# A list scheduler's hand-over times, and a choice of ScalarE or VectorE for each copy

## The chip, the cores and the metric

The kernel runs on one core of a Trainium2 chip. The time is that of the whole program on the device in microseconds (us), as a median over runs. The profile is of one execution.

## The reference

The program computes two transformer blocks, one after the other, on 512 tokens of width 1024 in float32. The first block has two layers; each is a feed-forward, a mixer, and a second feed-forward. The mixer of the first layer is an mLSTM with memory cross-attention, that of the second a dilated attention with memory cross-attention.

```python
for layer in range(DEPTH):
    x = x + 0.5 * swiglu(rms_norm(x, ffn1_norm[layer]), ...)
    h = rms_norm(x, mix_norm[layer])
    mix = mlstm_mixer(h, mem_n, ...) if layer < N_A_LAYERS else dilated_mixer(h, mem_n, k_sh, v_sh, ...)
    x = x + mix
    x = x + 0.5 * swiglu(rms_norm(x, ffn2_norm[layer]), ...)
```

The second block has two layers as well. Each scales and shifts its input by a learned modulation, projects it to everything that its three mixers need, and runs an RWKV recurrence in both directions, an attention with grouped heads and rotated queries and keys (with softmax), and an attention over neighbouring tokens. A context of 256 tokens goes through the same steps ahead of the 512.

```python
h_lat = x * (1.0 + scale[:, None]) + shift[:, None]
ru_l, rg_l, aq_l, ak_l, av_l, ag_l, nq_l, nk_l, nv_l, ng_l = jnp.split(h_lat @ w_in, SPLIT_POINTS, axis=-1)
_, _, ys_l = _rwkv_bidir(rin_l, S_f, S_b)                  # RWKV, both directions
gq_l = _apply_axial_rope(gqa_q(aq_l), cos, sin)            # rotated queries
ya_l = _block_attention(gq_l..., concat(gk_c, gk_l), concat(gv_c, gv_l))
yn_l = _neighbourhood_attention(nq_l, nk_l, nv_l, nk_c, nv_c, rpb)
y_l = concat([yr_l * silu(rg_l), ya_l * silu(ag_l), yn_l * silu(ng_l)]) @ w_out
x = _layer_norm(DEEPNORM_ALPHA * x + gate[:, None] * y_l, ln_g, ln_b)
```

## The kernel before

**Matrix products.** Activations lie with the channels on the 128 partitions and the 512 tokens along the free axis. Each float32 operand of a large product is split into a high and a low part; the three products high x high, high x low and low x high are added up in PSUM. A split is two instructions: a copy that rounds to the high part (ScalarE, `t<-raw` for weights), and a subtraction for the low part (VectorE, `t<-raw,t`). `raw` tiles are weights as loaded, `t` tiles hold 128x512 values, `ps` are the eight PSUM banks, `uv`, `S`, `big` and `tmp` belong to RWKV, and `s8`, `s16`, `s32`, `s64` are small tiles of scalars (the profile shows them as `s`).

**The program is a list first.** `Prog` runs through the two blocks and only records operations (`Op`): engine, method, operands. `weave` mixes the lists of parts that may run side by side: RWKV on the context beside the second feed-forward of the first block, and attention beside RWKV in each layer of the second block (`layer_mix`). `dependences` finds who must wait for whom. `schedule` then finds the order, and `emit` writes the instructions in that order. Since one line of `emit` issues everything, nearly every row of the profile names line 583; operations are told apart by engine, tile names and shapes.

**What sets the order.** `simulate` is a list scheduler. It keeps, for each of five engines, the time at which it comes free, and a time at which each operation is ready: the end of what it waits for plus `LATENCY` of that engine, plus `INTO_PE` if it is TensorE that waits. `_cost` gives each operation's length. At each step it takes the operation that can start first, by priority among those that are ready, and gives its tiles a free slot out of `SLOTS`. A change of TensorE's tile size is charged with `RETILE`, and on TensorE an operation of the same tile size may go ahead of others as long as their priorities lie within `STAY` us. `schedule` runs it backward through the program, takes the times as priorities for a run forward, and repeats this three times. On the chip each engine works through its own list in order and waits by semaphores; none of the planner's times reach the chip, only the order and the slots.

**Places that the prediction's steps touch.** `qstat` (lines 885 to 895) sums squares of a head on TensorE, reads the sums with a VectorE `TENSOR_SCALAR s<-ps` and raises them to -1/2 on GpSimd (`pow`). `heads` (808) spreads such numbers out again: a ScalarE copy `t<-s`, then TensorE transposes `ps<-const,t`. `roped` (1461) multiplies a query by a rotation matrix on TensorE; before that `attn_in` (1515) scales the query by a gain, a VectorE `TENSOR_SCALAR t<-t,const`. `attend` (1557) and `attn_run` (1523) are the softmax part. `rwkv_b` (1809) is a long chain of VectorE operations on `big` and `tmp` that solves a triangular system, `rwkv_d` (1861) the chain of small matmuls on `S` and `uv`. `split` and `loadw` (687, 696) make the high and low parts.

Of the kernel before, what the change touches and what calls it, by code (L numbers as in the profile page):

```python
# [13 lines left out]
AF = mybir.ActivationFunctionType  # L14
ALU = mybir.AluOpType
# [251 lines left out]
LATENCY = dict(tensor=0.22, vector=0.13, scalar=0.15, gpsimd=0.15, sync=3.0)  # L267
INTO_PE = 0.12
# [3 lines left out]
RETILE = 0.12  # L272
# [3 lines left out]
STAY = 2.0  # L276
# [82 lines left out]
class Op:  # L359
    def __init__(self, eng, method, a, k):  # L360
        self.eng, self.method, self.a, self.k = eng, method, a, k
        named = [(f"#{i}", x) for i, x in enumerate(a)] + list(k.items())
        refs = [(q in ("#0", "out", "accum_out"), x) for q, x in named if isinstance(x, Ref)]
        self.writes = [x for w, x in refs if w]
        self.reads = [x for w, x in refs if not w]
        self.tiling = self._tiling() if eng == "tensor" else None
        self.cost = self._cost()
# [7 lines left out]
    def _cost(self):  # L375

        n = max([x.cols() for x in self.writes + self.reads] or [1])
        ps = any(x.base.kind == "ps" for x in self.reads)
        if self.eng == "tensor":
            n = self.writes[0].cols()  # L380
            if self.method == "transpose":
                return 0.003 + 0.833e-3 * n
            if self.k["lhsT"].base.dt == F32R:
                return 0.0137 + n / 2400
            one = max(0.003 + n / 1200, 0.11 if self.tiling[1] == P else 0.08)
            return 2 * max(one / SIDE_BY_SIDE[self.tiling], 0.02)
        if self.eng == "vector":
            if self.method == "reciprocal":
                return 0.065 + 6.25e-3 * n
            fast = not ps and self.method in ("tensor_scalar", "tensor_copy", "memset")  # L390
            return 0.07 + n * (0.52e-3 if fast else 1.04e-3) + 0.06 * any(isinstance(self.k.get(q), Ref) for q in ("scalar", "scalar1"))
        if self.eng == "scalar":
            return (0.051 if ps else 0.094) + 0.833e-3 * n + 0.09 * ("accum_out" in self.k)
        if self.eng == "gpsimd":
            return 0.28 + 0.166 * n if self.k.get("op") == ALU.pow else 0.03 + (0.84e-3 if self.method == "memset" else 2.25e-3) * n
        return 0.05 + 1.65e-3 * n
# [55 lines left out]
def simulate(ops, before, after, key, lag, ahead):  # L452
# [9 lines left out]
    ready, free = [0.0] * n, dict.fromkeys(ENGINES, 0.0)  # L462
# [4 lines left out]
    for i in range(n):  # L467
        if not left[i]:
            heapq.heappush(wait[ops[i].eng], (0.0, i))
# [13 lines left out]

    def best(tight):
        out = None
        for e in ENGINES:
            limit = key[first[head]] + ahead(e)
            while wait[e] and wait[e][0][0] <= free[e]:
                i = heapq.heappop(wait[e])[1]
                heapq.heappush(can[e], (key[i], i))  # L490
            for src, time in ((can[e], lambda x: free[e]), (wait[e], lambda x: x[0])):
                pick = None
                for x in sorted(src):
                    i = x[1]
                    if key[i] > limit or pick and key[i] > pick[1] + STAY:
# [4 lines left out]
                    if pick and not same:  # L500
                        continue
# [11 lines left out]
    while len(order) < n:  # L513
# [10 lines left out]
        end = free[e] = at + ops[i].cost  # L524
# [8 lines left out]
        for j in after[i]:  # L533
            ready[j] = max(ready[j], end + lag(i, j))
            left[j] -= 1
            if not left[j]:
                heapq.heappush(wait[ops[j].eng], (ready[j], j))
    return order, slot, [start[i] + ops[i].cost for i in range(n)]


def schedule(ops):
# [16 lines left out]
    for _ in range(ROUNDS):  # L558
# [4 lines left out]
        out, key, far = ahead, [-x for x in ahead[2]], AGAIN  # L563
    return [ops[i] for i in out[0]], out[1]
# [1574 lines left out]
```

## Time and profile before

| what | value |
| --- | --- |
| median of 3 runs | 3243.61 us (3243.08 to 3245.81) |
| profiled execution | 3244.35 us |
| its span, first to last instruction | 3242.6 us |
| mean granted clock of TensorE, share of full speed | 0.982 |
| TensorE busy | 3127.8 us, 96% |
| VectorE busy | 2308.9 us, 71% |
| ScalarE busy | 1610.8 us, 50% |
| GpSimd busy | 269.8 us, 8% |
| DMA | 394.47 MB, mean 122 GB/s |

Busy times are sums over one engine's instructions. Engines work beside each other, so they do not add up to the span. PE is TensorE, PEld its weight loads, DVE VectorE, ACT ScalarE, POOL GpSimd and SP SyncE, which issues the DMAs. A wait is the idle time of an engine ahead of an instruction, with the engine and tile whose result ended it.

### The profile page before, as it was taken

How to read it: one execution, taken by the hardware profiler on the slowest of the kernel's cores; microseconds unless marked ns; L12 is line 12 of the kernel's file. 1: busy time of each engine (PE TensorE's matmuls, PEld its weight loads, DVE VectorE, ACT ScalarE, POOL GpSimd, SP SyncE). 2: the span in 40 equal slices, each digit the busy share in tenths (PEclk: the TensorE clock that was granted, in tenths of full speed). 3: DMA queues.
4: the chain of work that ended last, by engine and by line, in shares of the span. 5: the costliest groups of instructions: out<-in, count | busy, mean ns of one | idle time of the engine just before them, and what ended most of it. 6: DMA issues, size and time to landing. Idle time of an engine off the chain costs nothing.

```text
span 3242.6 us, 55887 instructions
## 1 busy us (share of the span) xinstructions
PE 3127.8 (96%) x21142; PEld 2581.6 (80%) x21142; DVE 2308.9 (71%) x4807; ACT 1610.8 (50%) x3589; POOL 269.8 (8%) x245
## 2 busy tenths in 40 slices
PE   8999999999999999999998999999999999998897
PEld 6788878878877889878886788887877778877777
DVE  9945686575688676687566756787677877577877
ACT  4333464463545254323346735443566854656863
POOL 1000000000001103000001000001211012011020
PEclk9999999999999999999999999999999999999998
DMA  6634432133433333355331333223544234544242
GB/s 232 202 108 127 133 110 88 56 103 116 141 102 116 116 130 111 100 180 159 120 104 58 115 105 110 83 90 97 174 142 156 87 110 135 163 143 148 80 133 83
DMA packets 205383, 394.47 MB, mean 122 GB/s; under 512 B 20789, under 2 KB 105397, under 8 KB 204985
## 3 DMA queue, kind: packets, MB, share of 16 engines
q1 hardware_dynamic: 205112, 390.90, 38.3%
q8 instruction: 166, 2.72, 0.3%
q14 instruction: 105, 0.85, 0.1%
HBM read 340.21 MB, written 48.24 MB: 120 GB/s over the span
## 4 chain that ended last, share of the span: by engine, by line
PE 80%; DVE 10%; ACT 5%; DMA 2%; issue 2%; POOL 1%; SPq 0%; ACTq 0%; POOLq 0%; DVEq 0%
PE ps L583 80%; DVE t L583 7%; ACT t L583 4%; ACT big L583 1%; DVE s L583 1%; DVE big L583 1%; ACT uv L583 1%; DVE tmp L583 1%; POOL s L583 1%; DMA t<-dram 1%; DMA raw<-in_wgu_dram 0%; DMA raw<-in_wmod_dram 0%; DMA dram<-t 0%; POOL uv L583 0%; DMA raw<-in_wout_dram 0%
## 5 line engine op out<-in xcount | busy, mean ns | idle before, releaser
L583 PE MATMUL ps<-t,t 128*128 128x512 f32 (+6 forms) x15204 | 2809.6, 351 | 44.6 <-DVE t L583 27.8
L583 PEld LDWEIGHTS ps<-t,t 128*128 128x128 f32 (+2 forms) x15204 | 2287.7, 183 | 475.5 <-issue 41.8
L583 ACT ACTIVATE t<-raw 128x512 fp32r<-128x512 f32 (+2 forms) x962 | 565.5, 612 | 776.2 <-PE ps L583 496.0
L583 DVE TENSOR_TENSOR t<-raw,t 128x512 fp32r<-128x512 f32 (+2 forms) x962 | 632.8, 674 | 310.0 <-PE ps L583 167.0
L583 ACT ACTIVATE t<-t 128x512 f32<-128x512 f32 (+10 forms) x749 | 378.0, 521 | 400.1 <-DVE t L583 204.0
L583 DVE TENSOR_TENSOR t<-t,t 128x256 f32<-128x256 f32 (+7 forms) x818 | 417.0, 540 | 92.9 <-ACT t L583 62.4
L583 ACT ACTIVATE t<-ps 128x512 f32<-128x512 f32 (+5 forms) x448 | 215.8, 512 | 212.1 <-PE ps L583 203.7
L583 DVE TENSOR_TENSOR t<-ps,t 128x512 f32<-128x512 f32 (+3 forms) x274 | 179.1, 658 | 159.7 <-PE ps L583 157.3
L583 POOL TENSOR_TENSOR s<-s,const 128x4 f32<-128x4 f32 (+6 forms) x65 | 111.1, 1711 | 1785.6 <-DVE s L583 1767.7
L583 PE MATMUL ps<-const,t 128*128 128x128 f32 (+1 forms) x1116 | 195.6, 295 | 38.6 <-ACT t L583 22.1
L583 PEld LDWEIGHTS ps<-const,t 128*128 128x128 f32 x1116 | 138.4, 150 | 83.0 <-ACT t L583 41.0
L583 DVE SCALAR_TENSOR_TENSOR t<-ps,t 128x512 f32<-128x512 f32 (+3 forms) x229 | 147.6, 649 | 51.5 <-PE ps L583 50.9
L583 ACT ACTIVATE t<-t,const 128x256 f32<-128x256 f32 (+3 forms) x165 | 101.5, 646 | 58.1 <-DVE t L583 25.2
L583 PE MATMUL ps<-uv,t 64*64 64x64 f32 (+1 forms) x2208 | 116.7, 230 | 5.0 <-DVE uv L583 4.4
L583 PEld LDWEIGHTS ps<-uv,t 64*64 64x64 f32 (+1 forms) x2208 | 93.2, 138 | 34.4 <-issue 15.2
L583 DVE SCALAR_TENSOR_TENSOR t<-raw,const,t 128x512 f32<-128x512 f32 x168 | 118.0, 752 | 1.8 <-DMA raw<-in_wmod_dram 1.8
L583 DVE SCALAR_TENSOR_TENSOR t<-t,t 128x512 f32<-128x512 f32 (+2 forms) x116 | 75.7, 655 | 49.9 <-ACT t L583 49.1
L583 ACT ACTIVATE uv<-ps 32x128 f32<-32x128 f32 (+1 forms) x288 | 92.5, 321 | 33.9 <-PE ps L583 29.9
L583 POOL TENSOR_TENSOR S<-S,s 128x192 f32<-128x192 f32 x96 | 57.1, 600 | 458.2 <-DVE S L583 390.2
L583 ACT ACTIVATE t<-ps,s,s 128x256 f32<-128x256 f32 (+1 forms) x140 | 88.6, 652 | 12.4 <-DVE s L583 12.1
L583 POOL TENSOR_TENSOR t<-t,s 64x512 f32<-64x512 f32 x36 | 52.1, 1459 | 481.0 <-DVE t L583 351.4
L583 DVE TENSOR_TENSOR big<-big,tmp 128x31 f32<-128x31 f32 (+15 forms) x248 | 84.6, 341 | 4.6
(81 smaller groups left out, 1406.2 us busy)
## 6 DMA issues: line engine op xcount, KB each, us to landing
raw<-in_wgu_dram SPq DMA_DIRECT2D x176, 512.0 KB, 3.6
raw<-in_win_dram SPq DMA_DIRECT2D x88, 512.0 KB, 4.0
raw<-in_wd_dram SPq DMA_DIRECT2D x128, 256.0 KB, 2.7
dram<-t SPq DMA_DIRECT2D x110, 256.0 KB, 2.2
raw<-in_wmod_dram SPq DMA_DIRECT2D x48, 512.0 KB, 4.1
t<-dram SPq DMA_DIRECT2D x179, 128.0 KB, 2.7
t<-dram SPq DMA_DIRECT2D x78, 256.0 KB, 3.0
dram<-t SPq DMA_DIRECT2D x114, 128.0 KB, 1.8
```

The source lines that it names most:

```text
L583: getattr(getattr(tc.nc, op.eng), op.method)(*map(real, op.a), **{q: real(v) for q, v in op.k.items()})
```

## The change

Numbers: every hand-over time of the planner is longer, `INTO_PE` goes from 0.12 to 0.5 us, a change of tile size is charged 0.14 for 0.12, `STAY` is 3 us for 2, and a GpSimd element costs 2.2 ns for 2.25.

Choice of engine: an operation may now have a second form on the other engine (`other`, with `costs` for both). A ScalarE copy, scaling, or scaling with an offset per partition has a VectorE form (`tensor_copy` or `tensor_scalar`); a VectorE `tensor_scalar` that multiplies, or multiplies and adds a tile, has a ScalarE form. Only outputs of 60 columns or more count (`SHARED`). `simulate` queues such an operation for both engines. The other engine takes it only if it would end over `MARGIN` = 1 us sooner there than behind what its own engine has queued ahead of it (`sooner`). After planning, `schedule` writes the chosen engine into the operation.

```diff
-LATENCY = dict(tensor=0.22, vector=0.13, scalar=0.15, gpsimd=0.15, sync=3.0)
-INTO_PE = 0.12
+LATENCY = dict(tensor=0.3, vector=0.2, scalar=0.25, gpsimd=0.5, sync=4.0)
+INTO_PE = 0.5
+SHARED = 60
+MARGIN = 1.0
...
-RETILE = 0.12
+RETILE = 0.14
...
-STAY = 2.0
+STAY = 3.0
...
+    def _others(self):
...
+        k = self.k
+        if self.eng == "scalar" and self.method == "activation" and "accum_out" not in k:
+            out, x, f = self.a
+            scale, bias = k.get("scale"), k.get("bias")
+            if out.cols() >= SHARED and (f == AF.Copy and bias is None or f == AF.Identity and isinstance(bias, Ref)):
+                if scale is None and bias is None:
+                    return ("vector", "tensor_copy", (out, x), {})
+                two = dict(scalar2=bias, op1=ALU.add) if bias is not None else dict(scalar2=None)
+                return ("vector", "tensor_scalar", (), dict(out=out, in0=x, scalar1=1.0 if scale is None else scale,
+                                                            op0=ALU.mult, **two))
+        if self.eng == "vector" and self.method == "tensor_scalar" and k["out"].cols() >= SHARED:
+            s, t = k["scalar1"], k["scalar2"]
+            if k["op0"] == ALU.mult and t is None:
+                return ("scalar", "activation", (k["out"], k["in0"], AF.Copy), dict(scale=s))
+            if k["op0"] == ALU.mult and k.get("op1") == ALU.add and isinstance(t, Ref):
+                return ("scalar", "activation", (k["out"], k["in0"], AF.Identity), dict(scale=s, bias=t))
+        return None
...
+    def sooner(i, e, at):
+
+        own = ops[i].eng
+        queue = sum(ops[j].costs[own] for k, j in can[own] if k < key[i] and not done[j])
+        return at + ops[i].costs[e] + MARGIN < max(free[own], ready[i]) + queue + ops[i].costs[own]
...
+                    if e != ops[i].eng and not sooner(i, e, time(x)):
+                        continue
...
-        end = free[e] = at + ops[i].cost
+        end = free[e] = at + ops[i].costs[e]
+        on[i] = e
...
+    for op, e in zip(ops, out[3]):
+        op.on(e)
```

The matmuls (17144), GpSimd instructions and DMAs stay the same in number. 126 operations go from ScalarE to VectorE: 30 high parts `t<-raw`, 49 copies `uv<-ps` of RWKV, 18 others out of PSUM, and the rest `t<-t`, 12 of them with factor and offset. 25 go the other way, 15 of them scalings of the modulation weights (`t<-raw,const`). The order on all engines is another throughout. Three places follow; the number in a name is that of the tile, and the number at the end the shape of the output.

First place: the first rotated query in the first `layer_mix`. On VectorE before, `s_5301` reads the sums of squares, `s_5310` comes after GpSimd's power, and `t_23872` is the query that is scaled by its gain:

```order
L583 TENSOR_SCALAR s_5301_23884<-ps_23876 128x8
L583 TENSOR_TENSOR big_22265<-big_22265,tmp_23911 128x7x25
L583 TENSOR_SCALAR s_5310_23913<-s_5303_23891 128x8
L583 TENSOR_TENSOR tmp_23919<-big_23608,big_22265 128x156
L583 TENSOR_SCALAR t_23872<-t_23872,const_90 128x512
L583 TENSOR_TENSOR big_22265<-big_22265,tmp_23919 128x6x26
L583 TENSOR_TENSOR tmp_23961<-big_23608,big_22265 128x135
```

On VectorE after, the step that reads the sums (`s_5259`) and the one after GpSimd's power (`s_5264`) stand with no query near them:

```order
L632 TENSOR_SCALAR s_5259_23685<-ps_23671 128x8
L632 TENSOR_TENSOR tmp_23705<-big_23540,big_22706 128x231
L632 TENSOR_SCALAR s_5264_23713<-s_5260_23689 128x8
L632 TENSOR_TENSOR t_23735<-raw_23632,t_23645 128x384
L632 TENSOR_TENSOR big_22706<-big_22706,tmp_23705 128x21x11
L632 TENSOR_TENSOR t_23744<-raw_23632,t_23647 128x384
L632 TENSOR_TENSOR tmp_23718<-big_23540,big_22706 128x240
```

On ScalarE after, the scaled query is `t_23855<-t_23855,const_90`:

```order
L632 ACTIVATE t_23855<-ps_23801 128x512
L632 ACTIVATE t_23906<-raw_23780 128x512
L632 ACTIVATE t_23865<-t_23855 128x512
L632 ACTIVATE t_23881<-ps_23616 128x384
L632 ACTIVATE t_23855<-t_23855,const_90 128x512
L632 ACTIVATE t_23892<-ps_23873 128x512
L632 ACTIVATE t_23896<-ps_23628 128x384
```

The scaling has gone from VectorE, where it stood two rows behind the step that takes GpSimd's result, to ScalarE, among copies.

Second place: TensorE ahead of the transposes of the head norms (`ps_28713<-const_239` before, `ps_28738<-const_214` after) in `layer_in` of the second layer. Before, these rows begin right behind the transposes of the sums that feed the chain:

```order
L583 MATMUL ps_28671<-t_28268,t_28289 128x512
L583 MATMUL ps_28671<-t_28279,t_28366 128x512
L583 MATMUL ps_28671<-t_28330,t_28306 128x512
L583 MATMUL ps_28671<-t_28279,t_28306 128x512
L583 MATMUL ps_28671<-t_28284,t_28366 128x512
L583 MATMUL ps_28671<-t_28336,t_28306 128x512
L583 MATMUL ps_28671<-t_28284,t_28306 128x512
L583 MATMUL ps_28671<-t_28315,t_28366 128x512
L583 MATMUL ps_28671<-t_28343,t_28306 128x512
L583 MATMUL ps_28671<-t_28315,t_28306 128x512
L583 MATMUL ps_28671<-t_28351,t_28366 128x512
L583 MATMUL ps_28713<-const_239,t_28704 128x128 x4
```

After, the same transposes of sums stand 22 matmuls of 128x512 ahead of the head norms' transposes; these are the last eleven of them:

```order
L632 MATMUL ps_28668<-t_28345,t_28239 128x512
L632 MATMUL ps_28668<-t_28323,t_28239 128x512
L632 MATMUL ps_28668<-t_28349,t_28352 128x512
L632 MATMUL ps_28668<-t_28361,t_28239 128x512
L632 MATMUL ps_28668<-t_28349,t_28239 128x512
L632 MATMUL ps_28723<-t_28234,t_28432 128x512
L632 MATMUL ps_28723<-t_28275,t_28289 128x512
L632 MATMUL ps_28723<-t_28234,t_28289 128x512
L632 MATMUL ps_28723<-t_28260,t_28432 128x512
L632 MATMUL ps_28723<-t_28279,t_28289 128x512
L632 MATMUL ps_28723<-t_28260,t_28289 128x512
L632 MATMUL ps_28738<-const_214,t_28728 128x128
```

Before, there are eleven matmuls between the two, after 22.

Third place: TensorE in RWKV's chain on the context, beside the feed-forward. `32x64` outputs on `S` and `64x64` outputs on `uv` are two tile sizes. Before:

```order
L583 MATMUL ps_10617<-S_8589,t_10200 32x64
L583 MATMUL ps_10619<-S_10390,t_10200 32x64
L583 MATMUL ps_10617<-uv_7764,t_10471 64x64
L583 MATMUL ps_10619<-uv_7764,t_10516 64x64
L583 MATMUL ps_10617<-uv_7764,t_10471 64x64
L583 MATMUL ps_10619<-uv_7764,t_10516 64x64
L583 MATMUL ps_10617<-uv_7764,t_10471 64x64
L583 MATMUL ps_10720<-S_10782,t_9627 32x64 x2
L583 MATMUL ps_10720<-S_10782,t_10276 32x64 x4
L583 MATMUL ps_10663<-uv_7740,t_8933 64x64 x2
L583 MATMUL ps_10663<-uv_7740,t_8952 64x64 x2
L583 MATMUL ps_10663<-uv_7740,t_8977 64x64 x2
```

After:

```order
L632 MATMUL ps_10643<-S_10729,t_9396 32x64 x4
L632 MATMUL ps_10643<-S_10729,t_9748 32x64 x2
L632 MATMUL ps_10737<-S_8702,t_10367 32x64
L632 MATMUL ps_10670<-S_10735,t_9748 32x64 x2
L632 MATMUL ps_10670<-S_10735,t_10281 32x64 x4
L632 MATMUL ps_10739<-S_10395,t_10367 32x64
L632 MATMUL ps_10737<-S_10395,t_10367 32x64
L632 MATMUL ps_10739<-S_8702,t_10367 32x64
L632 MATMUL ps_10737<-S_8702,t_10367 32x64
L632 MATMUL ps_10739<-S_10395,t_10367 32x64
L632 MATMUL ps_10651<-uv_7782,t_10377 64x64
L632 MATMUL ps_10653<-uv_7782,t_10400 64x64
```

The rows before change their tile size three times (to `uv`, back to `S`, and to `uv`), those after once.

## Rows read from the trace of the kernel before

**Rows 1.** The page: busy us, share and instructions by engine; then the chain's shares

```profile
PE 3127.8 (96%) x21142; PEld 2581.6 (80%) x21142; DVE 2308.9 (71%) x4807; ACT 1610.8 (50%) x3589; POOL 269.8 (8%) x245
PE 80%; DVE 10%; ACT 5%; DMA 2%; issue 2%; POOL 1%; SPq 0%; ACTq 0%; POOLq 0%; DVEq 0%
```

**Rows 2.** TensorE's waits: waiting tile, releaser, us in total, times, longest us

```profile
PE ps L583 <- DVE t L583: 53.5, 28, 13.4
PE ps L583 <- ACT t L583: 36.5, 39, 3.6
```

**Rows 3.** Busy us by stretch (attention with RWKV, twice; one piece); clock, DMA, GB/s

```profile
2365.00:2710.00 345.00, 322.72 (x3505) 261.34 (x3504) 275.44 (x646) 224.19 (x538) 53.59 (x59) 0.96 0.42 131
2840.00:3170.00 330.00, 306.80 (x3464) 248.06 (x3462) 260.48 (x610) 221.19 (x530) 46.82 (x52) 0.96 0.42 129
...
2480.00:2520.00 40.00, 35.11 (x340) 28.29 (x338) 37.28 (x69) 35.29 (x80) 6.58 (x5) 0.90 0.45 150
```

**Rows 4.** Timeline, first rotated query: start us, length us, engine, operation, [idle before <-releaser]

```profile
2439.26 0.17 DVE L583 TENSOR_SCALAR s<-s 128x8 f32<-128x8 f32 x1 [1.53 <-POOL s L583]
...
2439.57 0.48 DVE L583 TENSOR_SCALAR t<-t,const 128x512 f32<-128x512 f32 x1
...
2440.10 1.95 PE L583 MATMUL ps<-t,const 128*128 128x512 f32 x2 [2.90 <-DVE t L583]
```

**Rows 5.** Timeline, head norms of the second layer's input

```profile
2787.90 2.75 PE L583 MATMUL ps<-t,t 128*128 128x512 f32 x11
...
2788.45 4.17 POOL L583 TENSOR_TENSOR s<-s,const 128x24 f32<-128x24 f32 x1 [26.79 <-DVE s L583]
...
2792.64 0.63 ACT L583 ACTIVATE t<-s 128x512 f32<-128x512 f32 x1 [3.60 <-POOL s L583]
...
2793.33 0.66 PE L583 MATMUL ps<-const,t 128*128 128x128 f32 x4 [2.67 <-ACT t L583]
```

**Rows 6.** Timeline of TensorE: other gaps in the two stretches

```profile
2400.30 0.43 PE L583 MATMUL ps<-t,const 128*32 128x128 f32 x8 [1.94 <-ACT t L583]
...
2503.12 1.58 PE L583 MATMUL ps<-t,t 128*64 128x128 f32 x16 [1.73 <-DVE t L583]
...
2923.11 2.66 PE L583 MATMUL ps<-t,const 128*128 128x512 f32 x10 [3.67 <-DVE t L583]
...
3068.19 6.64 PE L583 MATMUL ps<-t,t 128*64 128x128 f32 x56 [1.66 <-DVE t L583]
```

**Rows 7.** Timeline of TensorE: small groups of RWKV on the context

```profile
1077.10 0.63 PE L583 MATMUL ps<-S,t 64*32 64x64 f32 x24
1077.66 0.80 PE L583 MATMUL ps<-uv,t 128*64 128x64 f32 x10
...
1082.31 0.53 PE L583 MATMUL ps<-S,t 64*32 64x64 f32 x12
1082.76 0.56 PE L583 MATMUL ps<-uv,t 64*64 64x64 f32 x12
```

**Rows 8.** Groups by shape: operation, count | busy us, mean ns | idle before, releasers

```profile
L583 ACT ACTIVATE t<-raw 128x512 fp32r<-128x512 f32 x842 | 506.1, 626 | 669.5 <-PE ps L583 417.7 <-DMA raw<-in_wgu_dram 91.9 <-DMA raw<-in_wd_dram 51.3
L583 ACT ACTIVATE uv<-ps 32x256 f32<-32x256 f32 x144 | 53.9, 374 | 12.8 <-PE ps L583 10.6
...
L583 DVE CAST t<-t 64x512 fp32r<-64x512 f32 x12 | 4.9, 419 | 0.2
L583 DVE TENSOR_SCALAR t<-ps,s 128x256 f32<-128x256 f32 x20 | 9.4, 481 | 4.7 <-ACT t L583 2.7 <-PE ps L583 2.0
```

**Rows 9.** Timeline, start and tail

```profile
12.22 0.48 DVE L583 TENSOR_SCALAR t<-raw,const 128x512 f32<-128x512 f32 x1
...
13.36 2.93 PE L583 MATMUL ps<-t,t 128*128 128x512 f32 x6 [13.36 <-DVE t L583]
...
3231.89 1.01 PE L583 MATMUL ps<-const,t 128*128 128x1 f32 x4 [6.87 <-DVE t L583]
```

More of the change, by code (lines that the diff above doesn't have):

```diff
@@ L366, in __init__ @@
         self.tiling = self._tiling() if eng == "tensor" else None
-        self.cost = self._cost()
+        self.other = self._others()
+        self.costs = {eng: self._cost(eng, method)}
+        if self.other:
+            self.costs[self.other[0]] = self._cost(*self.other[:2])
+        self.cost = self.costs[eng]
     def _tiling(self):
@@ L373, in _tiling, with on, _cost @@
         return up(32 * l.v.shape[0]), up(l.cols())
-    def _cost(self):
+    def _others(self):
[16 more added lines that the diff above has]
+        return None
+    def on(self, eng):
+        if eng != self.eng:
+            self.eng, self.method, self.a, self.k = self.other
+        self.cost = self.costs[eng]
+    def _cost(self, eng, method):
         n = max([x.cols() for x in self.writes + self.reads] or [1])
         ps = any(x.base.kind == "ps" for x in self.reads)
-        if self.eng == "tensor":
+        if eng == "tensor":
             n = self.writes[0].cols()
-            if self.method == "transpose":
+            if method == "transpose":
                 return 0.003 + 0.833e-3 * n
@@ L386, in _cost @@
             return 2 * max(one / SIDE_BY_SIDE[self.tiling], 0.02)
-        if self.eng == "vector":
-            if self.method == "reciprocal":
+        if eng == "vector":
+            if method == "reciprocal":
                 return 0.065 + 6.25e-3 * n
-            fast = not ps and self.method in ("tensor_scalar", "tensor_copy", "memset")
+            fast = not ps and method in ("tensor_scalar", "tensor_copy", "memset")
             return 0.07 + n * (0.52e-3 if fast else 1.04e-3) + 0.06 * any(isinstance(self.k.get(q), Ref) for q in ("scalar", "scalar1"))
-        if self.eng == "scalar":
+        if eng == "scalar":
             return (0.051 if ps else 0.094) + 0.833e-3 * n + 0.09 * ("accum_out" in self.k)
-        if self.eng == "gpsimd":
-            return 0.28 + 0.166 * n if self.k.get("op") == ALU.pow else 0.03 + (0.84e-3 if self.method == "memset" else 2.25e-3) * n
+        if eng == "gpsimd":
+            return 0.28 + 0.166 * n if self.k.get("op") == ALU.pow else 0.03 + (0.84e-3 if method == "memset" else 2.2e-3) * n
         return 0.05 + 1.65e-3 * n
@@ L461, in simulate @@
     empty = {k: [(0.0, i) for i in range(m)] for k, m in SLOTS.items()}
-    ready, free = [0.0] * n, dict.fromkeys(ENGINES, 0.0)
+    ready, free, on = [0.0] * n, dict.fromkeys(ENGINES, 0.0), [op.eng for op in ops]
     wait = {e: [] for e in ENGINES}
@@ L468, in simulate @@
         if not left[i]:
-            heapq.heappush(wait[ops[i].eng], (0.0, i))
+            for e in ops[i].costs:
+                heapq.heappush(wait[e], (0.0, i))
     def room(i, tight):
@@ L489, in best @@
                 i = heapq.heappop(wait[e])[1]
-                heapq.heappush(can[e], (key[i], i))
+                if not done[i]:
+                    heapq.heappush(can[e], (key[i], i))
             for src, time in ((can[e], lambda x: free[e]), (wait[e], lambda x: x[0])):
@@ L494, in best @@
                     i = x[1]
+                    if done[i]:
+                        continue
                     if key[i] > limit or pick and key[i] > pick[1] + STAY:
@@ L500, in best @@
                     if pick and not same:
+                        continue
+                    if e != ops[i].eng and not sooner(i, e, time(x)):
                         continue
@@ L536, in simulate @@
             if not left[j]:
-                heapq.heappush(wait[ops[j].eng], (ready[j], j))
-    return order, slot, [start[i] + ops[i].cost for i in range(n)]
+                for x in ops[j].costs:
+                    heapq.heappush(wait[x], (ready[j], j))
+    return order, slot, [start[i] + ops[i].costs[on[i]] for i in range(n)], on
 def schedule(ops):
```

## The prediction, made before the changed kernel ran

> **What bounds the kernel now.** I read the busy shares and the chain first: TensorE is busy in 3127.8 of 3242.6 us and holds 80% of the chain that ended last [rows 1]. So a change that leaves every matmul in place can win in two ways only: fewer gaps on TensorE, or less time per matmul. TensorE's waits came next. Nearly all of them end on VectorE or ScalarE writing a `t` tile: 53.5 us in 28 waits and 36.5 in 39; with the smaller lines of that view the sum is about 105 us [rows 2]. Of the 53.5, 13.4 us is the start of the kernel [rows 9]. The table by stretch shows where the other engines are near their limit: in the two stretches of the second block where attention and RWKV run side by side (345 and 330 us) VectorE is busy 275.44 and 260.48 us, TensorE 322.72 and 306.80, and in one piece of 40 us VectorE has 37.28 and ScalarE 35.29 [rows 3]. Last I followed single gaps back in the timelines [rows 4 to 6], and looked at TensorE where it changes between tile sizes [rows 7].
>
> The sum is made against the profiled execution, 3244.35 us. The median of the three runs, 3243.61, lies 0.74 lower. A measurement of this kernel can tell about 0.2% (6.5 us) from no change.
>
> **The change part by part.** No matmul is added or removed, nor any DMA or GpSimd instruction. What changes is the order on every engine, and the engine of 151 copies and scalings: 126 go from ScalarE to VectorE, 25 back.
>
> (a) *Tile-size changes on TensorE.* Counted over the orders, TensorE goes from one tile size to another 866 times before and 760 after, 106 fewer. 48 of them lead into a matmul of the two stretches of attention with RWKV (481 before, 433 after). The third pair of fences shows how: three changes in twelve rows become one. What one costs: a group of 24 matmuls of 64*32 starts at 1077.10 and the next group at 1077.66, that is 0.56 us; one of 12 takes 0.45 (1082.31 to 1082.76) [rows 7]. Twelve matmuls more cost 0.11, so twelve cost 0.11 and 0.34 is left for the change itself. 106 x 0.34 = 36 us is the upper bound. The lower is 0: where TensorE then waits for its neighbours, a saved change is only waited out. Nearly half of the saved changes lie where VectorE and ScalarE are nearly full, so I take a little under half: **-16**.
>
> (b) *Gaps on TensorE.* The planner now reckons 0.2 us (VectorE) and 0.25 (ScalarE) after a result, and 0.5 more into TensorE (0.7 and 0.75, where it had 0.25 and 0.27), so it puts more matmuls between the step that feeds a chain and the one that waits for it. Three places, worked out:
> - Rotated queries: a gap of 2.90 at 2440.10. Its matmul needs a scaling of 0.48 by a constant, which VectorE begins at 2439.57. That scaling needs nothing late, but stands in VectorE's row behind a step that waited 1.53 for GpSimd [rows 4]. After, this scaling is on ScalarE (first pair of fences), not behind that step. The same place in the other layer shows 3.67 [rows 6]. Most of the two goes: -6.
> - Head norms: eleven matmuls start at 2787.90, while the chain GpSimd power (4.17 from 2788.45), ScalarE copy (0.63) ends at 2793.27, and TensorE waits 2.67 [rows 5]. After, 22 matmuls stand there (second pair). At 2.75 us for eleven they last 5.5, the chain 5.4: -2.5.
> - Sums behind ScalarE's row: 1.94 at 2400.30 [rows 6], and two like it; more matmuls stand before them too: -4.
>
> The softmax parts have twelve gaps over 0.5 us, from 1.73 at 2503.12 to 1.66 at 3068.19 [rows 6], some 18 us in all. There ScalarE and VectorE are both nearly full, so earlier issue helps little: a third, -6. Of the remaining waits (105 less 16 here, 18 there and 23 at start and tail, about 48) I take a sixth, -8: more matmuls stand in front of nearly every such step in the new order, but most are waits I did not trace. Together -26.5. A new order makes new waits, of which the trace of before shows none. Bounds: zero, and all that is won. I charge 40%: **-16** net.
>
> (c) *The moved copies.* Rows near to one on VectorE: 0.419 for a cast out of SBUF, 0.481 for a scaling out of PSUM [rows 8]. With 0.41 as a mean (many are narrower): 126 x 0.41 = 52 us more; 25 x 0.48 = 12 less; +40 for VectorE, which stands at 2308.9 of 3242.6 [rows 1]. ScalarE is relieved by about as much (30 splits at 0.626, 96 others near 0.42, less 25 coming in at 0.6: -44). As VectorE idles elsewhere, most of this is hidden by its own slack. Where it is full it is not: 34 of the copies, 14 us, lie in the two stretches of [rows 3]. I charge a fifth: **+3**; bounds 0 and 14.
>
> Most moved copies read PSUM: 49 into `uv` and 18 others. The rows put one on ScalarE at 0.374 (32x256) and the nearest on VectorE at 0.481, other shape and operands [rows 8]. The Trainium skill (Perfetto Trace Analysis, Optimizing Scalar/DVE Operations) speaks against these moves: it gives a fixed cost per instruction of about 125 ns for VectorE on PSUM against 51 for ScalarE. By that page 67 copies would cost 67 x 74 ns = 5 us more than they relieve, an estimate; all of it exposed, the sum would be 5 us higher; the rows' difference has the same sign.
>
> (d) *Start.* SyncE now loads the first gate weights seventh, ahead of the modulation weights (eighth before), and VectorE no longer has the modulation scalings in front of the first split. The last of these begins at 12.22 for 0.48, and the first matmul at 13.36 [rows 9]. The load stands one 512 KB transfer earlier. Between 0 and -3: **-1.5**. The tail (its gap of 6.87 at 3231.89 [rows 9]) keeps its order: 0.
>
> Sum: -16 - 16 + 3 - 1.5 = -30.5; 3244.35 - 30.5 = 3213.85, less 0.74 for the median: **3213 us**.
>
> **The rivals.**
> 1. *Larger gain.* Every saved change counts (-36) and no new waits come (-26.5), copies hidden (0), start -1.5: -64, **3180 us**. For it: TensorE is 96% busy, so a change of tile size mostly lies in its busy time. Against: nearly half of the saved changes lie where others are full.
> 2. *Given back.* The longer lead means results are asked for earlier, and eight PSUM banks and 64 `t` tiles must hold them longer; TensorE then waits for a free bank rather than for a result. With new waits as large as those removed in (b) (0), saved changes waited out (0), and (c) and (d) as above: 3244.35 + 3 - 1.5 - 0.74 = **3245 us**. For it: the softmax gaps already end on the engines that empty the banks. Against: those places are 18 of 105 us.
> 3. *VectorE becomes the bound* in the two stretches of attention with RWKV (slower). There it has 37.28 of 40 us at the worst [rows 3]; 34 copies x 0.41 = 14 us stand in front of the softmax's maxima and RWKV's chains, and TensorE waits for them. It decides as soon as VectorE has under 1 us of 40 idle; (a) and (b) are then waited out: 3244.35 + 14 + 1 - 0.74 = **3259 us**. For it: 37.28 is near. Against: over each stretch VectorE is busy 79 to 80%, and a copy is moved only if the planner sees it end over 1 us sooner.
>
> That the change does not do what it says is excluded by the orders: 151 steps changed engine, and every row list is rewritten.
>
> **How the numbers follow.** Forecast 0.58 (own range 3195 to 3235), larger gain 0.18, given back 0.13, VectorE bound 0.11. The first two are faster by over 0.2%, the third is the same, the fourth slower: 0.76, 0.13, 0.11. The range 3178 to 3252 takes in the case of larger gain but its lower end, and all of the given-back case; about 0.07 lies below, 0.08 above.
>
> **What would show it.** (a): matmul groups of 64*32 and 64*64 twice as long and fewer, TensorE's busy time down by 10 to 36 us at an equal count. (b): waits on VectorE and ScalarE down from 90 to about 75; no gap over 1 us at the first rotated query nor at the head norms of the second layer. (c): VectorE near 2348 us, ScalarE near 1567; waits on VectorE in the two stretches not larger. (d): first matmul near 11.9. I am wrong if TensorE's busy time stays at 3128 (then (a) was hidden or never cost it), or if the waits stay near 105 at other places (rival 2), or if VectorE has over 39 of 40 us in pieces where TensorE waits for it (rival 3).

## The result, and the profile after

The changed kernel takes 3191.85 us (3188.24 to 3195.84), against 3243.35 for the kernel before in the same comparison: a ratio of 0.984 (95% interval 0.9823 to 0.9857), or 51.5 us less. The forecast was 3213, 30.5 us less. The profiled execution of after takes 3195.84 us, the longest of its four; its span is 3194.1, and against the span of before that is 48.5 us.

The busy line of the page of after, to set beside [rows 1]:

```profile
PE 3100.0 (97%) x21142; PEld 2581.2 (81%) x21142; DVE 2334.6 (73%) x4908; ACT 1567.7 (49%) x3488; POOL 267.4 (8%) x245
```

TensorE's busy time fell by 27.8 us at the same count of matmuls. The span less the busy time is TensorE's idle time: 3242.6 - 3127.8 = 114.8 before, 3194.1 - 3100.0 = 94.1 after, 20.7 less. The two sum to the 48.5. I call this idle time "gaps" from here on; the same subtraction is made for each experiment.

TensorE's waits of after, to set beside [rows 2] (waiting tile, releaser, us in total, times, longest):

```profile
PE ps L632 <- ACT t L632: 31.3, 33, 3.5
PE ps L632 <- DVE t L632: 31.3, 16, 11.6
PE ps L632 <- DVE s L632: 6.8, 3, 3.5
PE ps L632 <- POOL s L632: 4.7, 5, 1.4
PE ps L632 <- ACT uv L632: 4.1, 4, 2.7
PE ps L632 <- DVE uv L632: 1.4, 3, 0.5
```

The waits on `s` and `uv` tiles in the same view of before:

```profile
PE ps L583 <- DVE uv L583: 4.4, 6, 1.1
...
PE ps L583 <- POOL s L583: 3.0, 3, 1.2
PE ps L583 <- ACT uv L583: 1.4, 4, 0.7
PE ps L583 <- DVE s L583: 1.2, 1, 1.2
```

Waits on VectorE's `t` tiles went from 53.5 us in 28 to 31.3 in 16, those on ScalarE's from 36.5 to 31.3. Waits on `s` tiles grew from 4.2 to 11.5 us. Waits on `uv` tiles stayed, 5.8 us before and 5.5 after, but most of them now end on ScalarE. So new waits came, but smaller than what went.

The two stretches of attention with RWKV, as in [rows 3]; the start times have moved with the program:

```profile
2340.00:2680.00 340.00, 316.10 (x3609) 263.15 (x3608) 283.67 (x673) 214.78 (x517) 65.10 (x62) 0.97 0.42 132
...
2800.00:3122.00 322.00, 304.69 (x3459) 247.03 (x3457) 266.75 (x634) 209.17 (x501) 48.34 (x52) 0.97 0.41 129
```

As cut here, the stretches got 5 and 8 us shorter, with 8 and 6 us more of VectorE in them. VectorE is busy 83% there, 79 to 80% before. It is fuller on average; whether it became the bound is looked at under the rivals.

**Three places of the prediction.** The head norms of the second layer's input, as in [rows 5] (timeline: start, length, engine, operation, idle before):

```profile
2751.49 5.25 PE L632 MATMUL ps<-t,t 128*128 128x512 f32 x22
2756.81 1.42 PE L632 MATMUL ps<-const,t 128*128 128x128 f32 x11
...
2752.03 4.16 POOL L632 TENSOR_TENSOR s<-s,const 128x24 f32<-128x24 f32 x1 [24.21 <-DVE s L632]
```

The 22 matmuls are there, the power still takes 4.16 us, and the transposes at 2756.81 start with no gap; before they waited 2.67.

The first rotated query, as in [rows 4]:

```profile
2416.85 1.02 PE L632 MATMUL ps<-t,const 128*128 128x512 f32 x2
...
2423.43 0.17 DVE L632 TENSOR_SCALAR s<-s 128x8 f32<-128x8 f32 x1 [2.18 <-POOL s L632]
```

The step that waits for GpSimd still waits, now 2.18 us, but the rotation at 2416.85 is long done: its scaling no longer stands behind that step. The 2.90 us is gone.

The sums behind ScalarE's row, as the 1.94 of [rows 6]:

```profile
2829.41 3.11 ACT L632 ACTIVATE big<-ps 32x128 f32<-32x128 f32 x8
...
2832.54 0.28 ACT L632 ACTIVATE t<-ps 128x128 f32<-128x128 f32 x1
...
2832.87 0.33 PE L632 MATMUL ps<-const,t 128*128 128x128 f32 x1 [3.29 <-ACT t L632]
```

This kind of wait stayed: eight copies of RWKV (3.11 us) now stand on ScalarE ahead of the small copy that TensorE needs, and the gap is 3.29.

**New waits**, at places where before had none of over 2 us:

```profile
2347.32 2.54 POOL L632 TENSOR_TENSOR t<-t,s 64x512 f32<-64x512 f32 x2 [3.81 <-DVE t L632]
2347.40 3.00 DVE L632 TENSOR_TENSOR t<-t,s 64x512 f32<-64x512 f32 x2
...
2351.12 1.39 PE L632 MATMUL ps<-t,const 128*128 128x512 f32 x2 [3.33 <-DVE t L632]
...
2487.76 1.59 PE L632 MATMUL ps<-t,t 128*128 128x64 f32 x9 [3.12 <-DVE s L632]
...
2891.65 0.63 ACT L632 ACTIVATE t<-raw 128x512 fp32r<-128x512 f32 x1 [4.13 <-DMA raw<-in_win_dram]
...
2894.84 1.65 PE L632 MATMUL ps<-t,t 128*128 128x64 f32 x4 [2.70 <-ACT uv L632]
```

The first is the rotated key, whose gain is applied on VectorE behind two long products. These took 1.54 and 1.53 us beside two products of GpSimd; the ten of this shape in the kernel after that ran beside no GpSimd instruction took 0.67 to 0.68 each. The second is a matmul whose PSUM bank came free only when VectorE's maximum had read it. The third is RWKV's: its `uv` copy stood on ScalarE behind weight splits and other copies, and ScalarE had itself waited 4.13 us for weights before them.

**Tile-size changes.** Counted over TensorE's rows of the trace, tile sizes change 866 times before and 760 after. A step runs here from the start of one matmul to the start of the next, less the idle time. TensorE's busy time in the steps that lead into another size falls from 189.8 to 163.3 us, and in all other steps from 2937.6 to 2936.3. So nearly the whole fall in busy time lies in the steps between sizes, which are 106 fewer.

### The profile page after: what moved, and what is told of

Read it like the earlier page. It is cut to its first block, busy times and chain, and to the rows that moved or that the text cites. A ratio compares the mean times of both kernels' runs of the same rounds, so it can differ in the third digit from the quotient of the medians.

```text
span 3194.1 us, 55844 instructions
## 1 busy us (share of the span) xinstructions
PE 3100.0 (97%) x21142; PEld 2581.2 (81%) x21142; DVE 2334.6 (73%) x4908; ACT 1567.7 (49%) x3488; POOL 267.4 (8%) x245
## 5 line engine op out<-in xcount | busy, mean ns | idle before, releaser
L632 PE MATMUL ps<-t,t 128*128 128x512 f32 (+7 forms) x15204 | 2805.5, 351 | 40.4 <-ACT t L632 17.2
L632 PEld LDWEIGHTS ps<-t,t 128*128 128x128 f32 (+3 forms) x15204 | 2296.4, 184 | 459.9 <-issue 37.6
L632 ACT ACTIVATE t<-raw 128x512 fp32r<-128x512 f32 (+1 forms) x932 | 547.9, 612 | 759.8 <-PE ps L632 466.2
L632 ACT ACTIVATE t<-ps 128x512 f32<-128x512 f32 (+7 forms) x437 | 208.8, 513 | 179.7 <-PE ps L632 174.5
L632 PE MATMUL ps<-const,t 128*128 128x128 f32 (+1 forms) x1116 | 185.9, 286 | 27.3 <-ACT t L632 11.1
L632 ACT ACTIVATE t<-t,const 128x512 fp32r<-128x512 f32 (+3 forms) x155 | 96.3, 649 | 38.1 <-DVE t L632 27.6
L632 ACT ACTIVATE uv<-ps 32x128 f32<-32x128 f32 (+1 forms) x239 | 76.1, 320 | 38.4 <-PE ps L632 24.5
L632 ACT ACTIVATE t<-ps,const 128x256 f32<-128x256 f32 (+1 forms) x100 | 56.6, 576 | 71.9 <-PE ps L632 71.5
```

The lines of the kernel that those rows point to most:

```text
L632: getattr(getattr(tc.nc, op.eng), op.method)(*map(real, op.a), **{q: real(v) for q, v in op.k.items()})
```

## The experiments

Each is the kernel before or after with some lines changed, and each was run beside the kernel before on one chip. "Changes" are tile-size changes counted over the trace, "gaps" are the span less TensorE's busy time, both of the profiled execution. Times and ratios are of the whole comparison. "Theory" and "rival" are the two outcomes written down before the run.

**The parts alone.** First the tile numbers on the kernel before:

```diff
-RETILE = 0.12
+RETILE = 0.14
-STAY = 2.0
+STAY = 3.0
```

> The kernel before with only RETILE 0.14 and STAY 3 (hand-over times, INTO_PE and engines as before). The planner's own list has 680 changes of tile size here, 759 before and 702 after. Theory (tile sizes cost by themselves): TensorE busy falls by 20 to 28 us at the same count of matmuls and the gaps stay near 115 us, so 3215 to 3225 us. Rival (the busy time falls because of the longer hand-over times): TensorE busy stays near 3128, time within 6 us of 3243.

Measured: 3232.98 us, ratio 0.9964 (0.9952 to 0.9977). Changes 866 to 804, TensorE busy 3121.5, gaps 114.6. The mechanism is the theory's (busy time falls, gaps stay), the size is not: 62 fewer changes came with 6 us less busy time. The granted clock was 0.979 here and 0.982 before, which counts below.

Then the hand-over times on the kernel before:

```diff
-LATENCY = dict(tensor=0.22, vector=0.13, scalar=0.15, gpsimd=0.15, sync=3.0)
-INTO_PE = 0.12
+LATENCY = dict(tensor=0.3, vector=0.2, scalar=0.25, gpsimd=0.5, sync=4.0)
+INTO_PE = 0.5
```

> The kernel before with only the LATENCY values and INTO_PE of after (tile numbers and engines as before; 770 changes of tile size in the planner's list, 759 before). Theory (hand-over times shorten the gaps): gaps on TensorE fall by 15 to 25 us, TensorE busy stays at 3120 to 3130, so 3218 to 3230 us. Rival (the gaps fell through the choice of engine): gaps stay near 115 us, time within 6 us of 3243.

Measured: 3233.80 us, 0.9963 (0.9948 to 0.9978). Gaps 105.9, 9 less, short of the 15; busy 3128.7. The result lies between theory and rival.

Then the choice of engine with every number of before (the kernel after with the numbers set back):

```diff
-LATENCY = dict(tensor=0.3, vector=0.2, scalar=0.25, gpsimd=0.5, sync=4.0)
-INTO_PE = 0.5
+LATENCY = dict(tensor=0.22, vector=0.13, scalar=0.15, gpsimd=0.15, sync=3.0)
+INTO_PE = 0.12
-RETILE = 0.14
+RETILE = 0.12
-STAY = 3.0
+STAY = 2.0
-            return 0.28 + 0.166 * n if self.k.get("op") == ALU.pow else 0.03 + (0.84e-3 if method == "memset" else 2.2e-3) * n
+            return 0.28 + 0.166 * n if self.k.get("op") == ALU.pow else 0.03 + (0.84e-3 if method == "memset" else 2.25e-3) * n
```

> Only the choice of ScalarE or VectorE, with every number of before (109 operations move to VectorE, 29 to ScalarE; 776 changes of tile size in the planner's list, 759 before). Theory (the choice itself is worth little): within 8 us of 3243. Rival (the choice takes away the gaps): gaps fall by 15 us or more, 3228 us or less. Second rival (VectorE becomes the bound): slower, 3250 us or more, VectorE waits longer in the two stretches of attention with RWKV.

Measured: 3229.76 us, 0.9955 (0.9938 to 0.9972). It is faster by more than the theory of "worth little" allows, and short of the rival. Gaps 110.9, 4 less, of which 3 us are the earlier start of the first matmul (10.47 against 13.36); busy 3120.5 with 819 changes. The kernel is not slower, as it would be with VectorE as the bound.

**Two parts together.** The kernel after without the choice of engine:

```diff
-SHARED = 60
+SHARED = 100000
```

> The kernel after with the choice of engine switched off, all numbers of after (715 changes of tile size in the planner's list, 702 after). Theory (numbers bring the gain): 3190 to 3203 us, within 10 us of after. Rival (the choice brings 15 us or more of it): 3207 us or more.

Measured: 3217.55 us, 0.9916 (0.9902 to 0.9931), as the rival has it. The busy line of its page:

```profile
PE 3098.0 (96%) x21142; PEld 2578.2 (80%) x21142; DVE 2303.7 (72%) x4807; ACT 1605.5 (50%) x3589; POOL 261.3 (8%) x245
```

TensorE's busy time is as low as in after (756 changes), but the gaps are 3215.2 - 3098.0 = 117.2, no smaller than before. With the numbers alone none of the gap time goes.

The kernel after without the tile numbers:

```diff
-RETILE = 0.14
+RETILE = 0.12
-STAY = 3.0
+STAY = 2.0
```

> The kernel after with RETILE 0.12 and STAY 2 as before, and the rest of the change (784 changes of tile size in the planner's list, 702 after). Theory (0.26 us for each change of tile size): 60 to 90 more changes, TensorE busy 16 to 24 us more, gaps as after, 3205 to 3218 us. Rival (tile numbers do little beside longer hand-over times): within 7 us of after, 3199 us or less.

Measured: 3239.94 us, 0.9993 (0.9983 to 1.0002), nearly the kernel before and slower than both theory and rival. 856 changes and busy 3125.9, 26 us more than after (16 to 24 expected), but gaps of 120.6 that were not expected.

The kernel after without the hand-over times:

```diff
-LATENCY = dict(tensor=0.3, vector=0.2, scalar=0.25, gpsimd=0.5, sync=4.0)
-INTO_PE = 0.5
+LATENCY = dict(tensor=0.22, vector=0.13, scalar=0.15, gpsimd=0.15, sync=3.0)
+INTO_PE = 0.12
```

> The kernel after with the hand-over times and INTO_PE of before (choice of engine and tile numbers as after; 667 changes of tile size in the planner's list, 702 after). Theory (longer hand-over times are what shortens the gaps): gaps on TensorE 15 us or more above after's 94, the saved changes of tile size stay, 3200 us or more. Rival (tile numbers and choice of engine do it, the hand-over times add nothing): 3183 to 3197 us.

Measured: 3219.71 us, 0.9933 (0.9918 to 0.9948), as the theory has it. 783 changes, gaps 112.8. The eight combinations, medians in us (before measured 3244.7, 3242.8 and 3240.4 in the three comparisons that they come from; the cells marked * have GpSimd's 2.2 ns of after, the others 2.25):

| | no choice of engine | with the choice |
| --- | --- | --- |
| numbers of before | 3243 | 3230 |
| tile numbers | 3233 | 3220* |
| hand-over times | 3234 | 3240* |
| both | 3218* | 3192* |

Against the kernel before in the same comparison the parts alone give 11 to 15 us each, some 37 in all; together 51. The hand-over times with the choice but without the tile numbers give nearly nothing. Whether the effects really fail to add up depends on how far a cell can be trusted, which comes next.

**How much is chance.** One number of the planner that should mean nothing, on the kernel before:

```diff
-            return 0.28 + 0.166 * n if self.k.get("op") == ALU.pow else 0.03 + (0.84e-3 if self.method == "memset" else 2.25e-3) * n
+            return 0.28 + 0.166 * n if self.k.get("op") == ALU.pow else 0.03 + (0.84e-3 if self.method == "memset" else 2.2e-3) * n
```

> The kernel before with one number of the planner changed that should mean nothing: a GpSimd element costs 2.2 ns instead of 2.25. Every order is found anew. Theory (an order that differs by chance is worth a few us): within 5 us of 3243. Rival (chance alone moves the time by as much as single parts of the change did, 11 to 15 us): over 8 us away from 3243, on either side.

Measured: 3253.28 us, 1.0031 (1.0019 to 1.0044), as the rival has it. Gaps 113.7, one less, but 890 changes and 11 us more busy time. A meaningless number moves this kernel by 10 us, as much as one part of the change does. So the cells of the table are to be read with about 10 us on either side, and three neighbours of after were run. The first has that same number set back:

```diff
-            return 0.28 + 0.166 * n if self.k.get("op") == ALU.pow else 0.03 + (0.84e-3 if method == "memset" else 2.2e-3) * n
+            return 0.28 + 0.166 * n if self.k.get("op") == ALU.pow else 0.03 + (0.84e-3 if method == "memset" else 2.25e-3) * n
```

> The kernel after with one number that should mean nothing set back: a GpSimd element costs 2.25 ns instead of 2.2 (678 changes of tile size in the planner's list, 702 after). Theory (the gaps that went are won by the planner's numbers and choice, whatever order comes out): gaps 88 to 100 us, time within 8 us of 3192. Rival (the order of after is a lucky one): gaps 105 us or more, 3203 us or more.

Measured: 3203.30 us, 0.9880 (0.9864 to 0.9897). 780 changes, gaps 101.1: the rival's time, with gaps between the two. The second:

```diff
-RETILE = 0.14
+RETILE = 0.13
```

> The kernel after with RETILE 0.13 instead of 0.14 (683 changes of tile size in the planner's list, 702 after), a second neighbour. Theory (the gain is a property of the numbers): gaps 88 to 100 us, time within 8 us of 3192. Rival (the order of after is a lucky one): gaps 105 us or more, 3203 us or more.

Measured: 3210.30 us, 0.9901 (0.9887 to 0.9916). 749 changes, gaps 108.4, as the rival has it. The third:

```diff
-LATENCY = dict(tensor=0.3, vector=0.2, scalar=0.25, gpsimd=0.5, sync=4.0)
+LATENCY = dict(tensor=0.3, vector=0.2, scalar=0.25, gpsimd=0.45, sync=4.0)
```

> The kernel after with GpSimd's hand-over time at 0.45 us instead of 0.5 (719 changes of tile size in the planner's list, 702 after; 140 operations to VectorE, 25 to ScalarE), a third neighbour. Theory (the gain is a property of the numbers): gaps 88 to 100 us, time within 8 us of 3192. Rival (the order of after is a lucky one): gaps 105 us or more, 3203 us or more.

Measured: 3222.71 us, 0.9943 (0.9923 to 0.9963). 801 changes, gaps 99.2, busy 3128.8 at a clock of 0.976. Its gaps are the theory's, its time the rival's. Its four executions are not alike: 3217 and 3219 us at a granted clock of 0.983 and 0.982, 3227 and 3230 at 0.978 and 0.976. One and the same program was granted different clocks, and some 10 us of its time go with that.

All three are faster than before, and all three slower than after. The mean of the four orders is (3192 + 3203 + 3210 + 3223) / 4 = 3207 us. Each against the kernel before in its own comparison, they are 51.5, 37.1, 30.1 and 17.7 us faster, 34 on average, with gaps of 101 on average (94 to 108), 14 less. So some 34 us belong to the change as such (28 by the three neighbours alone), and after's further 17 to its being the best of these four orders: luck, as far as they show.

This also limits what the table shows. The kernel without the choice is 27 us faster than before in its own comparison, the one without the hand-over times 21. That is 7 and 13 less than the 34, about what the meaningless number moves, and both lie within the spread of the four orders. Only the kernel without the tile numbers, 3 us faster, lies outside it. And 37 us for the parts alone against 34 for the whole change add up well enough: no interplay of the parts is shown.

**Whether the engines matter or the order found with them.** The kernel after with its order and every operation back on its own engine:

```diff
-    for op, e in zip(ops, out[3]):
-        op.on(e)
```

> The kernel after with its order, but every operation back on the engine of before (126 back to ScalarE, 25 back to VectorE). Theory (the gaps fell because ScalarE and VectorE are relieved where they are late): gaps on TensorE rise by 15 us or more, 3207 us or more. Rival (the order found with the choice is what helps, whoever does the copy): within 7 us of after, 3185 to 3199 us. In both, TensorE's busy time stays near 3100 us.

Measured: 3212.79 us, 0.9909 (0.9894 to 0.9924), which is also within the spread of the neighbours. The time is the theory's, the reason is not: gaps rose only to 99.9, and TensorE's busy time rose by 14 us. (TensorE's rows are not quite those of after, though the planner's order is the same: 778 changes.) Matched by their number, the matmuls of the two profiled executions start within about 3 us of each other up to the 16500th, at 2680 us. They are 8 us apart at the 17500th and 5 at the 18000th, at 2916 us. By the 18500th, 60 to 75 us later, they are 19 us apart, and at the end 20. Both kernels there, by pieces (us; busy time of TensorE, weight loads, VectorE, ScalarE, GpSimd; then TensorE's granted clock). First with engines undone, then after:

```profile
2940.00:2960.00 20.00, 15.99 (x103) 12.78 (x102) 18.01 (x39) 15.32 (x37) 2.94 (x2) 0.71 0.26 79
2960.00:2980.00 20.00, 18.42 (x92) 14.41 (x92) 8.63 (x20) 14.32 (x35) 2.11 (x2) 0.50 0.13 42
2980.00:3000.00 20.00, 20.00 (x208) 17.87 (x208) 10.28 (x25) 11.45 (x27) 1.50 (x1) 0.68 0.24 86
```

```profile
2936.00:2956.00 20.00, 15.79 (x114) 11.50 (x113) 18.89 (x40) 18.30 (x47) 3.35 (x3) 0.91 0.23 74
2956.00:2976.00 20.00, 20.00 (x239) 17.17 (x239) 15.68 (x38) 17.28 (x43) 2.61 (x3) 0.83 0.15 49
2976.00:2996.00 20.00, 17.60 (x136) 12.89 (x134) 19.65 (x58) 15.89 (x43) 0.00 (x0) 1.00 0.28 93
```

VectorE and ScalarE have room in the first kernel (8.63 and 14.32 of 20 us), so no engine is short. The clock is: 0.50 over a whole piece, that is 1.2 GHz throughout, while TensorE did 92 matmuls in place of 239. Only 1.2 and 2.4 GHz were granted, so these pieces hold 2 x 20 x (0.29 + 0.50 + 0.32) = 44 us at 1.2 GHz with engines undone, and 2 x 20 x (0.09 + 0.17) = 10 in after. TensorE's timeline as it falls, engines undone and then after:

```profile
2943.81 2.24 PE L630 MATMUL ps<-t,t 128*64 128x128 f32 x18 [0.34 <-ACT t L630]
2946.93 0.73 PE L630 MATMUL ps<-t,t 128*128 128x512 f32 x2 [0.87 <-DVE t L630]
2948.64 1.11 PE L630 MATMUL ps<-const,t 128*128 128x128 f32 x4 [0.98 <-ACT t L630]
2949.55 3.10 PE L630 MATMUL ps<-t,t 128*128 128x64 f32 x14
```

```profile
2939.12 2.24 PE L632 MATMUL ps<-t,t 128*64 128x128 f32 x18 [0.33 <-ACT t L632]
2942.24 0.73 PE L632 MATMUL ps<-t,t 128*128 128x512 f32 x2 [0.87 <-DVE t L632]
2943.95 0.66 PE L632 MATMUL ps<-const,t 128*128 128x128 f32 x4 [0.98 <-ACT t L632]
2944.71 1.77 PE L632 MATMUL ps<-t,t 128*128 128x64 f32 x14
```

The same matmuls with the same gaps (0.34, 0.87, 0.98): after them, the four small ones take 1.11 us in one kernel and 0.66 in the other. So in the profiled executions most of what undoing the engines costs lies in one place, and is the clock there. Up to 2680 us, having these copies on VectorE or on ScalarE made about 3 us at most. Why the clock fell there for 44 us in the one and for 10 in the other is open. Over the whole program it is lower in all four executions with engines undone (0.979 to 0.982) than in all four of after (0.984 to 0.988), but the third neighbour shows that it can also differ between executions of one program.

**The price of a tile-size change**, on purpose far out:

```diff
-STAY = 3.0
+STAY = 10.0
```

> The kernel after with STAY 10 instead of 3 (538 changes of tile size in the planner's list, 702 after). Theory (a change costs about 0.26 us of TensorE's busy time, as 26.5 us for 106 between before and after): 120 to 165 fewer changes, TensorE busy 30 to 43 us less, gaps up by at most 10 us, 3150 to 3175 us. Rival (matmuls of the same size that go ahead by up to 10 us hold up those that other engines wait for): gaps grow by 30 us or more, 3185 us or more.

Measured: 3189.99 us, 0.9837 (0.9822 to 0.9852), the same as after. The busy line of its page:

```profile
PE 3081.8 (97%) x21142; PEld 2578.7 (81%) x21142; DVE 2338.6 (73%) x4920; ACT 1565.8 (49%) x3476; POOL 273.5 (9%) x245
```

654 changes, 106 fewer than after, and 18 us less busy time; but gaps of 107.3, 13 more. What the one gives the other takes: fewer changes do save busy time, as the theory has it, and the time is the rival's. Over all fourteen profiled kernels, from 654 to 890 changes, a least-squares line through TensorE's busy time gives 0.24 us for each change and 0.34 us for each us at the lower clock (118 us of it in before, 107 in after, 131 here, 154 in the third neighbour), and misses single kernels by 6 us at most. Here it gives 106 x 0.24 = 25 us less for the changes and 24 x 0.34 = 8 more for the clock. For the tile numbers alone, with 141 us at the lower clock, it gives 15 less and 8 more, against the 6 less that were measured.

## Why the prediction held, and where it did not

**The direction and the two causes** were right: less time per matmul through fewer tile-size changes, and fewer gaps. The time lies in the range, between the forecast (3213) and the case of larger gain (3180), nearer to the latter and just below the forecast's own range (3195 to 3235). The three neighbours, 3203 to 3223, lie inside that; what took after beyond it is, as far as these show, the luck of its order.

**(a) Tile-size changes: too small.** I took 0.15 us a change, since nearly half of them lie where other engines are full. They are not waited out: 106 x 0.24 = 25 us, against my 16, and the busy time fell by 27.8. In the two stretches, cut as above, TensorE's busy time fell by 8.7 us and its idle time did not rise (45.5 before, 41.2 after). The upper end (0.34) was too high. My picture of where was wrong too: steps into 64*32 tiles fell only from 114 to 107 and into 64*64 not at all (128); the fall is into 128*64 (198 to 161) and 128*128 (340 to 291). The place shown for RWKV's small groups is real but not typical.

**(b) Gaps: near in sum, not in the parts.** With (c) and (d) the forecast was -14.5; after shows -20.7, and the mean of the four neighbouring orders -14. The signs came: waits on `t` tiles fell from 90 us to 63 (forecast 75). By function of the waiting matmul (each row of the trace put to the operation that it issues): head norms 3.5 to 1.3 us over the whole program (-2.2, forecast -2.5). In the two stretches: rotations 9.8 to 5.8 (-4, forecast -6, because the rotated key now waits); softmax 17.5 to 12.3 (-5.2, forecast -6); sums 5.4 to 5.3 (forecast -4: that step failed, ScalarE's row is as full of RWKV's copies as it was). New waits did come, RWKV's `uv` step (`rwkv_c`) most of all (4.9 to 9.8).

The prediction also misread two rows. The gaps at 2503.12 and 3068.19 [rows 6], which it gives as the first and last of the softmax's twelve, stand before matmuls of RWKV's `uv` step; with the one at 2987.13 they make 4.6 of its 18 us. Softmax and this step together lost nothing (22.4 us before, 22.1 after), where the prediction has -6 for the twelve.

So the places that were worked out, with the start and the `uv` step, make some 8 of the 20.7 us. The other 12 went where nothing was traced and -8 was taken: the softmax of the dilated attention fell from 5.3 to 0.0, the feed-forwards apart from the start of the kernel from 7.0 to 1.5, RWKV on the context (`ctx_out`) from 6.5 to 2.5. That the sum came out near is luck.

I put all of (b) to the longer hand-over times, and that is not shown. The gaps were 94 to 108 with the whole change, 117 for the numbers without the choice, 113 for the choice and tile numbers without the hand-over times, 121 without the tile numbers. They are lowest with all of it in place; but the hand-over times alone gave 106, inside the range of the whole change, so the merit cannot be split with one order each.

**(c) The moved copies: the cost is not seen.** I charged 3 us for VectorE. Its busy time rose by 25.7 us (forecast 40), ScalarE's fell by 43.1 (forecast 44). With the numbers set, adding the choice took 26 us off (3218 to 3192), but only 7 by the mean of the four orders; alone it took 15. So the sign speaks for a gain, of a size that one order cannot give. Nearly the same order with engines undone ran level for 2680 us, so no gain from the relief itself is seen there. The Trainium skill's rule on PSUM (Perfetto Trace Analysis, Optimizing Scalar/DVE Operations) has the direction right: the same copy is dearer on VectorE. The 74 ns between its two figures are an upper end here; the rows show 420 ns for 32x256 against 374 on ScalarE [rows 8]:

```profile
L632 DVE COPY uv<-ps 32x256 f32<-32x256 f32 x15 | 6.3, 420 | 1.9 <-ACT uv L632 1.6
```

At these 46 ns the copies out of PSUM cost some 3 us more than they relieve, an estimate; nothing of that size can be told from the spread of orders. (The trace has 68 of them on VectorE, not 67, and three of the moved copies that were put down as `t<-t` read small `s` tiles.)

**(d) Start.** First matmul at 11.59 for 13.36, 1.8 us earlier (forecast 1.5, "near 11.9"). The tail kept its gap of 6.87 us.

**The rivals.** New waits in the place of old came as the second rival has it, a PSUM bank freed late among them (3.12 at 2487.76), but smaller than the gain. VectorE as the bound did not come: the two stretches got 5 and 8 us shorter. Its sign, over 39 of 40 us on VectorE in a piece, does not tell: a piece like that stood in the kernel before as well. The fullest pieces of the stretches, before and then after (TensorE first, VectorE third):

```profile
2534.00:2574.00 40.00, 38.23 (x452) 31.84 (x450) 39.07 (x107) 34.87 (x88) 0.00 (x0) 1.00 0.26 81
```

```profile
2971.00:3011.00 40.00, 37.50 (x405) 30.34 (x404) 39.28 (x102) 31.95 (x78) 1.05 (x1) 1.00 0.30 95
```

The sum of this rival also adds 1 us for which the prediction gives no source.

What the prediction lacked is the spread of orders: 10 us from a meaningless number. Its bounds came out of costs of single steps, and held because those were wide.

## What to carry to other kernels

Where a list scheduler sets the order, run two or three neighbours (a number that should mean nothing) before any part is given credit: here after and its neighbours spread over 31 us, and a part alone was worth 11 to 15. Count TensorE's tile-size changes, since they are busy time that no wait table shows: 0.24 us each here. When the busy time of TensorE rises at an equal count of matmuls and of tile changes, look at the granted clock by stretch before any engine is blamed.

## What was not expected of the hardware

Two programs with the same matmuls and the same three gaps (0.34, 0.87 and 0.98 us) were granted different clocks behind them, and the one that stayed at 1.2 GHz for 44 us in place of 10 lost some 15 us within 80.

A copy moved to VectorE can be held up by GpSimd. The kernel after has two VectorE copies of a small `s` tile spread over a `t` tile of 128x512, and one takes nearly seven times as long as the other:

```profile
2290.36 5.54 POOL L632 MEMSET uv<- 32x3072 f32 x2
...
2290.46 2.84 DVE L632 COPY t<-s 128x512 f32<-128x512 f32 x1 [3.48 <-POOL s L632]
...
2756.23 0.43 DVE L632 COPY t<-s 128x512 f32<-128x512 f32 x1 [3.02 <-POOL s L632]
```

The long one runs beside a `MEMSET` of GpSimd and ends 0.3 us after the first of the two. Over all kernels with this copy, the six that overlap these `MEMSET`s take 2.84 us (five) and 1.06 us (one), and those that overlap none take 0.42 to 0.43. ScalarE's mean for the same shape in the kernel after is 0.63:

```profile
L632 ACT ACTIVATE t<-s 128x512 f32<-128x512 f32 x16 | 10.0, 634 | 11.5 <-POOL s L632 11.3 <-DVE s L632 0.2
```

So the copy is shorter on VectorE when GpSimd is idle and much longer when it is not, and the planner's formula for it, which goes by columns and by PSUM alone, does not know that. The two long products ahead of the rotated key at 2351.12 show the same.
